# Sliding attention of a decoder layer: keys and values reversed by blocks, the sink as a 129th score, two output halves joined from PSUM

## The chip, the core and the metric

The kernel runs on one core of a Trainium2 chip. A core has five engines with a queue of instructions each: TensorE (PE, matrix products, with its weight loads listed as PEld), VectorE (DVE), ScalarE (ACT), GpSimd (POOL) and SyncE (SP), which here issues all DMA transfers. Each queue is worked off in order; an instruction whose data or buffer isn't ready holds those behind it. The metric is the time of one execution on the device, in microseconds.

## The reference, cut to what matters

One decoder layer, 1024 tokens, width 1024, everything in float32: a norm, input projections, two token mixers side by side (sliding attention and gated linear attention), gates, output projections, residual, norm. The change lies in the sliding attention, with 16 query heads of 64, 2 key heads, blocks of 128 queries and a window of 128:

```python
s = jnp.einsum('bnqhgd,bnkhd->bnhgqk', qb, keys).astype(jnp.float32) * (A_HEAD_DIM ** -0.5)
...
rel = qi + BLOCK - ki
band = (rel >= 0) & (rel < WINDOW)
valid = band[None] & ((blk > 0) | (ki >= BLOCK)[None])
s = jnp.where(valid[None, :, None, None], s, NEG_INF)
...
p = jax.nn.softmax(jnp.concatenate([s, sink], axis=-1), axis=-1)[..., :-1]
o = jnp.einsum('bnhgqk,bnkhd->bnqhgd', p.astype(v.dtype), vals)
```

`keys` holds 256 keys for a block of queries: those of the block before and its own. Of these, 128 are in the window of each query: for query q the own keys 0 to q, and q + 1 to 127 of the block before. Key 0 of the block before is in no query's window. The sink is one learned number per head that stands in the softmax's sum and has no value.

## The kernel before, in words

All products are float32 made of rounded parts: an operand x is h (x rounded) and l (the rest), and a product is h*h + h*l + l*h. The layer runs as one program: norm and transposes, projections that are parked in DRAM (in blocks of 512, on banks `sj`), then the sliding attention (the `with ExitStack() as c2` block, L564 to L734), then the gated linear attention, the output projections and the last norm. The order within each engine's queue is set when the program is built: a scheduler puts the instructions in an order by its own estimate of when each can start, so instructions of one unit of attention stand among projections and other units.

The attention works through 8 pairs of heads `i`. `prep` (L719) makes the next pair's queries and gates: weights come in by DMA, ACT rounds them to `wh` (L115), POOL subtracts to `wl` (L116), PE projects (`proj`, L132), POOL turns the queries (`rope`, L585 to L587), ACT and DVE split them into `qa`, `qb` (L639 to L642); `silu2` makes the gate `ag` (L293). `attend` (L645) then takes two halves `th` of 512 tokens, and in each two units `u` of two blocks `b`: 32 units in all. A unit is:

- PE: scores of two blocks for two heads into banks `sc` (three of them), 256 keys wide (L659). Queries carry h and l on the two halves of the partitions, keys are doubled.
- DVE: per block, a select that puts at each place after the query's the score of the block before (L665), in place in PSUM, and the maximum over the 128 places (L666).
- DVE: per block, nm = min(-max / 8, -sink) (L673) and nm + sink (L675), two columns each; ACT: the exponential of that (L676), and four exponentials of 128 scores with nm as bias, 1/8 as scale and a sum (L678).
- DVE: the sink's part is added to the sum (L680), and the reciprocal taken (L681). ACT scales two of the four score tiles (L685), DVE two (L687).
- PE: four transposes into the bank `pt` (one, L688). ACT rounds them to `ph` (L695), DVE subtracts to `pl` (L697), POOL masks both with the causal triangle to `ch` and `cl` (L696, L698).
- PE: the products with the values into `av` (two banks, L704). Values carry h on 64 output partitions and l on the other 64, so the result has two halves that must be added: ACT copies one (L707), DVE adds the other (L708), and DVE multiplies by 1/4 and the gate, one head at a time, into `oa` (L712), which goes to DRAM (L717).

With one key head for eight query heads, `kk[g]` holds the keys of head g, h and l, 1024 columns in the order of the tokens (L591 to L602). For the first block there is no block before, and the select takes -1e30.

Of the kernel before, what the change touches and what calls it, by code (L numbers as in the profile page):

```python
# [25 lines left out]
P = 128  # L26
# [31 lines left out]
def _turn_parts(k):  # L58
    """1/(2 pi) * 2**k modulo 1 as (multiple of 2**-12, rest)."""
    from fractions import Fraction  # L60

    pi = Fraction(314159265358979323846264338327950288419716939937510582097494459, 10**62)
    f = Fraction(2**k) / (2 * pi)
    f -= round(f)
    hi = Fraction(round(f * 4096), 4096)
    return float(hi), float(f - hi)
# [3 lines left out]
def layer_kernel(ctx: ExitStack, tc: tile.TileContext, consts, x, positions, norm_w, w_in, a_sinks,  # L70
# [56 lines left out]
    def half_product(p, w, m, start, stop):  # L127
        """p (+)= w^T m over 512 rows, both split."""
# [6 lines left out]
    def proj(w, m):  # L135
        """[128 columns of w, 512 tokens] of w^T m."""
# [20 lines left out]
    # hT[token half][row half]: (h, l)  # L157
# [109 lines left out]
    # the norm's weights, by head the same, with the factors of the queries and of the halves  # L267
# [19 lines left out]
    def silu2(pool, name, w, th, bufs=None):  # L287
        """2 silu of the projection's tile."""
# [65 lines left out]
    nsinks = const.tile([P, AH], F32, name="nsinks")  # L354
    nc.vector.tensor_scalar_mul(nsinks, sinks, -1.0)
# [5 lines left out]
    # the sums at the middle and end of the blocks  # L361
# [9 lines left out]
    # ---- pairs of column tiles over blocks of 512 x 512, seven half products instead of eight:  # L371
    # with W^T = [[a11, a12], [a21, a22]] by tile and row half, and the other operand in blocks bij,
    # s1 = a21 + a22, s2 = s1 - a11, s3 = a11 - a21, s4 = a12 - s2,
    # t1 = b12 - b11, t2 = b22 - t1, t3 = b22 - b12, t4 = b21 - t2,
    # u2 = a11 b11 + s2 t2, c11 = a11 b11 + a12 b21, c21 = u2 + s3 t3 + a22 t4,
    # c22 = u2 + s3 t3 + s1 t1, c12 = u2 + s1 t1 + s4 b22 ----
    slots = []

    def part(raw, n):
        """h and l of raw [P, 4, n]."""  # L380
# [12 lines left out]
    def token_product(p, w, m, t):  # L393
        """p = m^T w over 512 rows for token tile t of the half, both split."""
# [649 lines left out]
```

## Time and profile before

| | |
|---|---|
| time, median of 3 runs | 1153.88 us (1153.28 to 1154.51) |
| profiled execution, span (its own time isn't given apart) | 1153.5 us |
| busy in the span: PE, PEld, DVE, ACT, POOL | 1048.5, 885.6, 824.2, 535.7, 701.8 us |
| first select (L665) to the start of the last output product (L712) | 474.9 to 769.1 us |
| mean granted clock of PE | 0.969 |

The page of the profile gives busy times, 40 slices of the span, and groups of instructions as "line engine operation out<-in, shapes, count | busy us, mean ns | idle before, and who ended it". A view of one line adds "min/median/max" of the durations. A window's row gives the busy time of each engine in a stretch, with the number of instructions in brackets. In a timeline the columns are start, duration, engine, line. A wait's row names who waited for whom: total us, times, longest. A DVE instruction that stands blocked once it has started counts as busy all the while.

### The profile page before, as it was taken

The numbers are of one execution on the slowest core, as the hardware profiler recorded it, in microseconds if no ns is written. First come the engines' busy times: TensorE is split into PE (matmuls) and PEld (weight loads), VectorE is DVE, ScalarE is ACT, GpSimd is POOL, SyncE is SP. The second block draws the span as 40 slices with busy tenths as digits, with TensorE's granted clock in tenths as the row PEclk, the third lists the DMA queues.
The fourth block names the chain that finished last, engine by engine and source line by source line (L and its number), as shares of the span: only waits on it lengthen the run. The fifth ranks groups of instructions, "written<-read, shape, count | busy, mean of one in ns | idle before, by whom it ended". The sixth has DMA issues, their size and how long they took to land.

```text
span 1153.5 us, 16395 instructions
## 1 busy us (share of the span) xinstructions
PE 1048.5 (91%) x5544; PEld 885.6 (77%) x5544; DVE 824.2 (71%) x1386; ACT 535.7 (46%) x1248; POOL 701.8 (61%) x554
## 2 busy tenths in 40 slices
PE   5797999989999999988999899988999997994897
PEld 4575878878889997877777787767788885874896
DVE  6893688535564323699999899957866289899766
ACT  6236675333342214455555554636755143333444
POOL 4545455777996437657556675557845144679585
PEclk9998999999999999999999999998999998996998
DMA  6303443453334152221221213246764488641325
GB/s 223 92 32 114 143 146 128 146 181 103 111 116 123 63 151 61 64 65 37 83 83 46 56 56 108 85 137 195 246 190 136 137 269 244 181 137 55 104 62 182
DMA packets 126403, 141.07 MB, mean 122 GB/s; under 512 B 10352, under 2 KB 87024, under 8 KB 126320
## 3 DMA queue, kind: packets, MB, share of 16 engines
q1 hardware_dynamic: 126320, 140.03, 39.2%
q8 instruction: 44, 0.72, 0.3%
q14 instruction: 39, 0.32, 0.1%
HBM read 95.04 MB, written 40.24 MB: 117 GB/s over the span
## 4 chain that ended last, share of the span: by engine, by line
PE 39%; DVE 24%; issue 5%; POOL 5%; ACT 3%; DMA 3%; SPq 0%; POOLq 0%; DVEq 0%; ACTq 0%
PE pj L132 12%; PE sj L397 12%; PE sj L132 10%; DVE oa L712 3%; DVE nm L673 2%; DVE sm L687 2%; DVE mx L666 2%; DVE pl L697 2%; DVE sc L665 1%; POOL wl L116 1%; PE av L750 1%; DVE qa L641 1%; DVE qb L642 1%; DVE fo L708 1%; DVE den L680 1%
## 5 line engine op out<-in xcount | busy, mean ns | idle before, releaser
L132 PE MATMUL pj<-o,wh 128*128 128x512 f32 x1088 | 359.4, 405 | 9.3 <-DVE low L308 6.0
L132 PEld LDWEIGHTS pj<-o,wh 128*128 128x128 f32 x1088 | 205.1, 193 | 51.3 <-issue 6.4
L116 POOL TENSOR_TENSOR wl<-wr,wh 128x1024 fp32r<-128x1024 f32 (+1 forms) x76 | 164.7, 2177 | 113.1 <-ACT wh L115 106.7
L132 PE MATMUL pj<-o,wl 128*128 128x512 f32 x544 | 218.1, 401 | 0.0
L116 POOL TENSOR_TENSOR wl<-sraw,wh 128x512 fp32r<-128x512 f32 (+1 forms) x98 | 153.9, 1587 | 92.8 <-ACT wh L115 84.9
L132 PEld LDWEIGHTS pj<-o,wl 128*128 128x128 f32 x544 | 104.6, 192 | 21.4
L132 PE MATMUL sj<-o,wh 128*128 128x512 f32 x352 | 112.6, 401 | 5.0 <-ACT wh L115 4.8
L115 ACT CAST wh<-wr 128x1024 fp32r<-128x1024 f32 (+1 forms) x76 | 66.6, 889 | 93.0 <-PE pj L132 29.0
L428 DVE TENSOR_TENSOR u<-u,sj 128x512 f32<-128x512 f32 x72 | 49.1, 684 | 74.6 <-PE sj L132 37.0
L115 ACT CAST wh<-sraw 128x512 fp32r<-128x512 f32 (+1 forms) x98 | 63.2, 678 | 65.1 <-PE sj L397 29.9
L132 PEld LDWEIGHTS sj<-o,wh 128*128 128x128 f32 x352 | 67.2, 191 | 21.5 <-ACT wh L115 5.1
L678 ACT ACTIVATE sm<-sc,nm 128x128 f32<-128x128 f32 x128 | 46.1, 365 | 76.8 <-DVE nm L673 64.5
L397 PE MATMUL sj<-wh,b 128*128 128x256 f32 x320 | 63.8, 301 | 18.8 <-ACT b L881 9.2
L696 POOL TENSOR_TENSOR ch<-ph,cst 128x512 fp32r<-128x512 f32 x32 | 38.7, 1211 | 54.9 <-ACT ph L695 54.9
L132 PE MATMUL sj<-o,wl 128*128 128x512 f32 x176 | 70.4, 400 | 0.0
L397 PEld LDWEIGHTS sj<-wh,b 128*128 128x128 f32 x320 | 54.3, 208 | 20.2 <-ACT b L881 9.6
L132 PE MATMUL sj<-b,wh 128*128 128x512 f32 x160 | 50.7, 401 | 7.2 <-ACT wh L115 7.2
L397 PE MATMUL sj<-wh,o 128*128 128x256 f32 x320 | 57.3, 282 | 0.0
L698 POOL TENSOR_TENSOR cl<-pl,cst 128x512 fp32r<-128x512 f32 x32 | 38.5, 1202 | 18.1 <-DVE pl L697 9.8
L397 PEld LDWEIGHTS sj<-wh,o 128*128 128x128 f32 x320 | 49.3, 188 | 0.1
L397 PE MATMUL sj<-wl,b 128*128 128x256 f32 x160 | 46.5, 298 | 2.3 <-POOL wl L116 2.3
L585 POOL TENSOR_TENSOR qs<-qs,sin 128x512 f32<-128x512 f32 x18 | 24.2, 1343 | 35.5 <-DMA qs<-q 25.0
(313 smaller groups left out, 2823.5 us busy)
## 6 DMA issues: line engine op xcount, KB each, us to landing
sraw<-in_w_in_dram SPq DMA_DIRECT2D x32, 512.0 KB, 4.0
wr<-in_w_in_dram SPq DMA_DIRECT2D x26, 512.0 KB, 3.9
r<-sp_ob SPq DMA_DIRECT2D x28, 256.0 KB, 4.5
qs<-q SPq DMA_DIRECT2D x72, 64.0 KB, 2.0
xt<-in_x_dram SPq DMA_DIRECT2D x8, 512.0 KB, 8.2
sp_ma<-gt SPq DMA_DIRECT2D x16, 256.0 KB, 2.1
sp_mb<-c SPq DMA_DIRECT2D x16, 256.0 KB, 2.0
gt<-sp_cum SPq DMA_DIRECT2D x16, 256.0 KB, 3.6
```

The lines of the kernel that those rows point to most:

```text
L115: nc.scalar.copy(h, raw)
L116: nc.gpsimd.tensor_sub(l, raw, h.bitcast(F32))
L132: nc.tensor.matmul(p, a[:, k, :], b[:, k, :], start=start and k == 0 and y == 0, stop=stop and k == 3 and y == 2)
L397: nc.tensor.matmul(p, m[i][:, k, t * P : t * P + P], w[j][:, k, :], start=k == 0 and y == 0, stop=k == 3 and y == 2)
L428: nc.vector.tensor_add(o[b], like(u[b], o[b]), like(x[b], o[b]))
L585: nc.gpsimd.tensor_mul(qs, qs, sin[:, sl])
L666: nc.vector.reduce_max(mx[:, 2 * b : 2 * b + 2], own, axis=mybir.AxisListType.X)
L673: nc.vector.scalar_tensor_tensor(nm[:, 2 * b : 2 * b + 2], mx[:, 2 * b : 2 * b + 2], -0.125, nsinks[:, h0 : h0 + 2], ALU.mult, ALU.min)
L678: nc.scalar.activation(sm[:, j, :], sel[j // 2][:, j % 2, :], AF.Exp, bias=nm[:, j : j + 1], scale=0.125, accum_out=den[:, j : j + 1])
L696: nc.gpsimd.tensor_mul(ch, ph.bitcast(F32), leb)
L698: nc.gpsimd.tensor_mul(cl, pl.bitcast(F32), leb)
L712: nc.vector.scalar_tensor_tensor(oa[o : o + 64, u * 256 : u * 256 + 256].rearrange("p (b q) -> p b q", b=2), fv[:, :, h, :], 0.25, ag[o : ...
```

## The change

The program outside the attention is the same but for removed comments and a tile `nsinks` that is no longer made. In the attention:

- Keys are stored with 1/8 folded in, and last block first, with a ninth block of zeros behind (`kk` is 9 x 128 columns). The 256 columns that a unit reads are then the own block first and the block before behind it. The four zero blocks are cleared by POOL.
- The place of key 0 of the block before, column 128, which no query uses, takes the sink: ACT copies two numbers per partition into the score bank. Own block and sink are then 129 columns side by side.
- The select works on places 1 to 127 (place 0 is always the own key). One reduction takes minus the maximum over 129 columns, the exponential runs over 129 columns without a scale, and its sum holds the sink's part. The operations on two and four columns (L673, L675, L676, L680) are gone.
- The output: for each head ACT copies one half, times 1/4, from PSUM, and DVE multiplies the other half by 1/4 and adds, into a tile `fo` of 128 x 256; one product by the gate follows for both heads.

```diff
-        kk = [[(aps if g else ap0).tile([P, T], F32R, name=f"k{g}{x}") for x in "hl"] for g in range(AKV)]
+        kk = [[(aps if g else ap0).tile([P, NT + 1, P], F32R, name=f"k{g}{x}") for x in "hl"] for g in range(AKV)]
+        for g in range(AKV):
+            for y in range(2):
+                nc.gpsimd.memset(kk[g][y][:, NT, :].bitcast(F32), 0.0)
...
-            r = rope(w, th)
+            r = rope(w, th).rearrange("p (n t) -> p n t", n=4)[:, ::-1, :]
+            sl = slice(NT - 4 - th * 4, NT - th * 4)
...
-                    nc.scalar.copy(kk[g][0][o2 : o2 + 64, sl], r[o : o + 64, :])
+                    nc.scalar.activation(kk[g][0][o2 : o2 + 64, sl, :], r[o : o + 64], AF.Copy, scale=AD**-0.5)
...
-                    nc.vector.tensor_sub(kk[g][1][o2 : o2 + 64, sl], r[o : o + 64, :],
-                                         kk[g][0][o : o + 64, sl].bitcast(F32))
+                    nc.vector.scalar_tensor_tensor(kk[g][1][o2 : o2 + 64, sl, :], r[o : o + 64], AD**-0.5,
+                                                   kk[g][0][o : o + 64, sl, :].bitcast(F32), ALU.mult, ALU.subtract)
...
-                    k0 = max(n - 1, 0) * P
+                    k0 = NT - 1 - n
...
-                    sv = s.rearrange("p (h w j) -> p h w j", h=2, w=2)
-                    own = sv[:, :, min(n, 1), :]
-                    nc.vector.copy_predicated(own, up, sv[:, :, 0, :] if n else neg[:, :, None].to_broadcast([P, 2, P]))
-                    nc.vector.reduce_max(mx[:, 2 * b : 2 * b + 2], own, axis=mybir.AxisListType.X)
+                    sv = s.rearrange("p (h j) -> p h j", h=2)
+                    nc.scalar.copy(sv[:, :, P], sinks[:, h0 : h0 + 2])
+                    nc.vector.copy_predicated(sv[:, :, 1:P], up[:, :, 1:], sv[:, :, P + 1 :] if n else
+                                              neg[:, :, None].to_broadcast([P, 2, P - 1]))
+                    own = sv[:, :, : P + 1]
+                    nc.vector.tensor_reduce(nm[:, 2 * b : 2 * b + 2], own, axis=mybir.AxisListType.X,
+                                            op=ALU.max, negate=True)
...
-                for b in range(2):
-                    nc.vector.scalar_tensor_tensor(nm[:, 2 * b : 2 * b + 2], mx[:, 2 * b : 2 * b + 2], -0.125,
-                                                   nsinks[:, h0 : h0 + 2], ALU.mult, ALU.min)
-                    nc.vector.tensor_add(sk[:, 2 * b : 2 * b + 2], nm[:, 2 * b : 2 * b + 2], sinks[:, h0 : h0 + 2])
-                nc.scalar.activation(sk, sk, AF.Exp)
...
-                                         scale=0.125, accum_out=den[:, j : j + 1])
-                nc.vector.tensor_add(den, den, sk)
+                                         accum_out=den[:, j : j + 1])
...
-                fo = ap.tile([64, 512], F32, name="fo", bufs=2)
-                nc.scalar.copy(fo, av[64:128, :])
-                nc.vector.tensor_add(fo, av[0:64, :], fo)
-                fv = fo.rearrange("p (b h q) -> p b h q", b=2, h=2)
+                fo = ap.tile([P, 256], F32, name="fo", bufs=2)
+                avv = av.rearrange("p (b h q) -> p h b q", b=2, h=2)
+                fv = fo.rearrange("p (b q) -> p b q", b=2)
+                us = slice(u * 256, u * 256 + 256)
                 for h in range(2):
-                    o = h * 64
-                    nc.vector.scalar_tensor_tensor(
...
-                        ALU.mult, ALU.mult)
+                    o, o2 = slice(h * 64, h * 64 + 64), slice(64 - h * 64, P - h * 64)
+                    nc.scalar.activation(fv[o], avv[o2, h], AF.Copy, scale=0.25)
+                    nc.vector.scalar_tensor_tensor(fv[o], avv[o, h], 0.25, fv[o], ALU.mult, ALU.add)
+                nc.vector.tensor_mul(oa[:, us], fo, ag[:, us])
```

The scheduler makes a new order from this. On DVE, some way into the attention, a unit's work ran like this before (`sc` scores, `mx` maximum, `nm` minus the maximum, `sk` and `den` the sink's part and the sum, `sm` the probabilities, `pl` the rest of their rounding, `fo` and `oa` the output; lines as in the kernel before):

```order
L665 COPY_PREDICATED sc<-up,sc 128x2x128
L697 TENSOR_TENSOR pl<-pt,ph 128x512
L666 TENSOR_REDUCE mx<-sc 128x2
L673 SCALAR_TENSOR_TENSOR nm<-mx,nsinks 128x2
L675 TENSOR_TENSOR sk<-nm,sinks 128x2
L708 TENSOR_TENSOR fo<-av,fo 64x512
L712 SCALAR_TENSOR_TENSOR oa<-fo,ag 64x256 x2
L680 TENSOR_TENSOR den<-den,sk 128x4
L293 SCALAR_TENSOR_TENSOR ag<-gt,pj 128x512
L681 RECIPROCAL den<-den 128x4
L687 TENSOR_SCALAR sm<-sm,den 128x128 x2
L697 TENSOR_TENSOR pl<-pt,ph 128x512
```

And now, about as far along in DVE's queue of the changed kernel (L671 select, L674 maximum, L713 multiply-add of the halves, L714 product by the gate, L680 reciprocal, L686 scaling, L696 subtraction for `pl`):

```order
L671 COPY_PREDICATED sc<-up,sc 128x2x127
L713 SCALAR_TENSOR_TENSOR fo<-av,fo 64x256
L674 TENSOR_REDUCE nm<-sc 128x2
L713 SCALAR_TENSOR_TENSOR fo<-av,fo 64x256
L714 TENSOR_TENSOR oa<-fo,ag 128x256
L680 RECIPROCAL den<-den 128x4
L686 TENSOR_SCALAR sm<-sm,den 128x128 x2
L293 SCALAR_TENSOR_TENSOR ag<-gt,pj 128x512
L696 TENSOR_TENSOR pl<-pt,ph 128x512
```

The maximum itself is what ACT waits for now; nothing stands between it and the exponential, nor between sum and reciprocal. The output's two multiply-adds stand apart, with a maximum between them.

On ACT, for a unit inside the attention, with what each waits for in brackets (an engine's or a DMA queue's semaphore), before (`ph` the rounded probabilities, L707 the copy of the output half, L291 the gate):

```order
L707 COPY fo<-av 64x512 [waits PE_49]
L695 CAST ph<-pt 128x512 [waits PE_49]
L678 ACTIVATE sm,den<-sc,nm 128x128 [waits DVE_49,Activation_49]
L678 ACTIVATE sm,den<-sc,nm 128x128
L678 ACTIVATE sm,den<-sc,nm 128x128 [waits DVE_49]
L678 ACTIVATE sm,den<-sc,nm 128x128
L291 ACTIVATE gt<-pj 128x512 [waits PE_49]
L676 ACTIVATE sk<-sk 128x4 [waits DVE_49]
L685 ACTIVATE sm<-sm,den 128x128 [waits DVE_49,Activation_49]
L685 ACTIVATE sm<-sm,den 128x128 [waits Activation_49]
```

And now (L670 the sink's copy into the score bank, L712 the copy of an output half, L684 the scaling, L694 the rounding):

```order
L670 COPY sc<-sinks 128x2 [waits PE_49]
L712 ACTIVATE fo<-av 64x256 [waits PE_49]
L678 ACTIVATE sm,den<-sc,nm 128x129 [waits DVE_49,Activation_49]
L678 ACTIVATE sm,den<-sc,nm 128x129
L291 ACTIVATE gt<-pj 128x512 [waits PE_49]
L712 ACTIVATE fo<-av 64x256 [waits DVE_49]
L678 ACTIVATE sm,den<-sc,nm 128x129 [waits DVE_49,Activation_49]
L678 ACTIVATE sm,den<-sc,nm 128x129
L684 ACTIVATE sm<-sm,den 128x128 [waits DVE_49]
L684 ACTIVATE sm<-sm,den 128x128 [waits Activation_49]
L694 CAST ph<-pt 128x512 [waits PE_49]
```

The sink's copy waits for PE's scores and stands ahead of what follows in the queue, and the second half's copy waits for DVE, whose multiply-add of the first half is to be done with the bank.

More of the change, by code (lines that the diff above doesn't have):

```diff
@@ L352, in layer_kernel @@
             nc.sync.dma_start(sp_rope[i, :, g * 256 : g * 256 + 256], trig[i][g * 32 : g * 32 + 32, :])
-    nsinks = const.tile([P, AH], F32, name="nsinks")
-    nc.vector.tensor_scalar_mul(nsinks, sinks, -1.0)
     caus = const.tile([P, P], I32, name="caus")
@@ L588, in rope @@
             return q
-        kk = [[(aps if g else ap0).tile([P, T], F32R, name=f"k{g}{x}") for x in "hl"] for g in range(AKV)]
+        kk = [[(aps if g else ap0).tile([P, NT + 1, P], F32R, name=f"k{g}{x}") for x in "hl"] for g in range(AKV)]
+        for g in range(AKV):
+            for y in range(2):
+                nc.gpsimd.memset(kk[g][y][:, NT, :].bitcast(F32), 0.0)
         w = wtile(w_in, O_AK)
         for th in range(TH):
-            sl = slice(th * 512, th * 512 + 512)
-            r = rope(w, th)
+            r = rope(w, th).rearrange("p (n t) -> p n t", n=4)[:, ::-1, :]
+            sl = slice(NT - 4 - th * 4, NT - th * 4)
             for g in range(AKV):
@@ L649, in attend @@
             for u in range(2):
-                mx = ap.tile([P, 4], F32, name="mx")
+                nm = ap.tile([P, 4], F32, name="nm")
+                den = ap.tile([P, 4], F32, name="den")
+                sm = ap.tile([P, 4, P + 1], F32, name="sm", bufs=2)
                 sel = []
@@ L658, in attend @@
                         for x in range(2):
-                            nc.tensor.matmul(s[:, h * 256 : h * 256 + 256], lq, kk[kv][x][:, k0 : k0 + 256],
+                            nc.tensor.matmul(s[:, h * 256 : h * 256 + 256], lq,
+                                             kk[kv][x][:, k0 : k0 + 2, :].rearrange("p n t -> p (n t)"),
                                              start=x == 0, stop=x == 1)
-                    sv = s.rearrange("p (h w j) -> p h w j", h=2, w=2)
-                    own = sv[:, :, min(n, 1), :]
@@ L665, in attend @@
-                    nc.vector.copy_predicated(own, up, sv[:, :, 0, :] if n else neg[:, :, None].to_broadcast([P, 2, P]))
-                    nc.vector.reduce_max(mx[:, 2 * b : 2 * b + 2], own, axis=mybir.AxisListType.X)
-                    sel.append(own)
-                nm = ap.tile([P, 4], F32, name="nm")
-                sk = ap.tile([P, 4], F32, name="sk")
-                den = ap.tile([P, 4], F32, name="den")
-                sm = ap.tile([P, 4, P], F32, name="sm", bufs=2)
-                for b in range(2):
-                    nc.vector.scalar_tensor_tensor(nm[:, 2 * b : 2 * b + 2], mx[:, 2 * b : 2 * b + 2], -0.125,
-                                                   nsinks[:, h0 : h0 + 2], ALU.mult, ALU.min)
-                    nc.vector.tensor_add(sk[:, 2 * b : 2 * b + 2], nm[:, 2 * b : 2 * b + 2], sinks[:, h0 : h0 + 2])
@@ L684, in attend @@
                     if j < 2:
-                        nc.scalar.activation(sm[:, j, :], sm[:, j, :], AF.Copy, scale=den[:, j : j + 1])
+                        nc.scalar.activation(sm[:, j, :P], sm[:, j, :P], AF.Copy, scale=den[:, j : j + 1])
                     else:
-                        nc.vector.tensor_scalar_mul(sm[:, j, :], sm[:, j, :], den[:, j : j + 1])
-                    nc.tensor.transpose(pt[:, j * P : j * P + P], sm[:, j, :], ident)
+                        nc.vector.tensor_scalar_mul(sm[:, j, :P], sm[:, j, :P], den[:, j : j + 1])
+                    nc.tensor.transpose(pt[:, j * P : j * P + P], sm[:, j, :P], ident)
                 parts = [ap.tile([P, 4, P], F32R, name=nm_, bufs=2) for nm_ in ("ph", "pl", "ch", "cl")]
```

3 lines of the change are left out of this document (removed).

## The prediction

> **What bounds the kernel now.** I read the page's 40 slices first, then the stage in which the changed lines run (476 to 770 us) beside two stretches in which PE is full, then the groups of DVE in that stage, single lines, and two places in the timeline.
>
> ```profile
> PE   5797999989999999988999899988999997994897
> DVE  6893688535564323699999899957866289899766
> core 0: us, PE busy (x) PEld busy (x) DVE busy (x) ACT busy (x) POOL busy (x), PEclk, DMA share, GB/s
> 280.00:320.00 40.00, 40.00 (x176) 32.73 (x175) 22.74 (x31) 15.57 (x29) 33.83 (x23) 1.00 0.35 114
> 360.00:400.00 40.00, 40.00 (x338) 40.00 (x337) 14.36 (x18) 9.60 (x11) 17.62 (x8) 1.00 0.33 104
> 476.00:770.00 294.00, 267.54 (x1396) 220.38 (x1395) 265.04 (x561) 160.53 (x496) 176.65 (x130) 0.99 0.24 71
> ```
>
> A slice is 28.8 us; from the 18th slice to the 26th DVE stands at 8 or 9 tenths. The stage has 294 us; DVE is busy in 265.0 of them (90%), PE in 267.5 (91%), so the page alone does not say which of the two sets the time. Two more views do: the chain that ended last, asked for this stage alone, and the waits.
>
> ```profile
> by line: DVE oa L712 12.6%; DVE nm L673 7.9%; DVE sm L687 7.8%; PE pj L132 7.2%; DVE mx L666 6.4%; DVE pl L697 6.2%; issue 6.0%; DVE sc L665 5.8%; DVE qa L641 5.0%; DVE qb L642 4.9%; DVE fo L708 4.7%; DVE den L680 4.6%; DVE sk L675 4.5%; DV
> ACT sm L678 <- DVE nm L673: 64.5, 32, 4.9
> ACT sm L685 <- DVE den L681: 25.3, 16, 3.3
> PE av L704 <- ACT ph L695: 9.9, 8, 3.0
> PE pt L688 <- DVE pl L697: 6.3, 7, 2.3
> ```
>
> Eleven of the thirteen entries that can be read in the chain are DVE's, PE's projections have 7.2%, and the longest wait (64.5 us, 32 times) is ACT waiting for a maximum that DVE makes. DVE sets this stage.
>
> How much room PE has is a matter of how it is read. In a full stretch 176 matmuls 512 columns wide take 40.00 us, 0.227 us each, and 338 that are 256 wide 0.118 us each. Four transposes follow each other like this:
>
> ```profile
> 571.11 0.60 PE L688 MATMUL pt<-cst,sm 128*128 128x128 f32 x4
> 571.46 0.48 PE L132 MATMUL pj<-o,wh 128*128 128x512 f32 x1
> L132 PE MATMUL pj<-o,wh 128*128 128x512 f32 x522 | 171.5, 401 | 0.1
> L132 PE MATMUL pj<-o,wl 128*128 128x512 f32 x262 | 104.5, 399 | 0.0
> L688 PE MATMUL pt<-cst,sm 128*128 128x128 f32 x128 | 24.5, 287 | 10.7 <-DVE pl L697 6.3 <-DVE sm L687 3.2 <-ACT sm L685 0.9
> ```
>
> The next matmul starts 0.35 us after the first of the four: 0.088 us each. The stage's 1396 PE instructions are 784 wide ones (522 + 262), 128 transposes and 484 others, all 256 wide: 784 x 0.227 + 484 x 0.118 + 128 x 0.088 = 178.2 + 57.3 + 11.2 = 246.7 us. So PE needs 247 of the 294 us, and 47 us is the most that the stage can give.
>
> Weighed against a page: the busy column leaves PE only 26.5 us of room (294 - 267.5), the starts leave 47, because a matmul's bar is longer than the distance to the next. The Trainium skill (Perfetto Trace Analysis, Identifying the Most-Contended Engine) calls matmul busy time no good measure and takes the share of weight loads instead; these are busy 220.4 of 294 us here (75%) and 32.7 to 40.0 of 40 where PE is full, so the trace sides with it. By the busy column the forecast below would be 26.5 - 20.6 = 6 us of gain and 1148 us.
>
> **What DVE's time consists of.** Its groups in the stage that the change touches, then their spread (min/median/max, ns):
>
> ```profile
> L712 DVE SCALAR_TENSOR_TENSOR oa<-fo,ag 64x256 f32<-64x256 f32 x64 | 41.4, 647 | 0.7
> L687 DVE TENSOR_SCALAR sm<-sm,den 128x128 f32<-128x128 f32 x64 | 32.4, 547 | 0.8
> L673 DVE SCALAR_TENSOR_TENSOR nm<-mx,nsinks 128x2 f32<-128x2 f32 x64 | 27.1, 427 | 0.8
> L675 DVE TENSOR_TENSOR sk<-nm,sinks 128x2 f32<-128x2 f32 x64 | 24.6, 390 | 0.5
> L708 DVE TENSOR_TENSOR fo<-av,fo 64x512 f32<-64x512 f32 x32 | 21.6, 675 | 7.9 <-ACT fo L707 7.7
> L680 DVE TENSOR_TENSOR den<-den,sk 128x4 f32<-128x4 f32 x32 | 15.3, 478 | 5.7 <-ACT sk L676 5.1
> L641 DVE TENSOR_TENSOR qa<-q,qa 64x512 fp32r<-64x512 f32 x14 | 14.7, 1049 | 2.6 <-ACT qa L639 2.2
> L673 DVE SCALAR_TENSOR_TENSOR nm<-mx,nsinks x64: 124/160/2284, 477.4 to 751.7; 128x2 f32<-128x2 f32 x64
> L675 DVE TENSOR_TENSOR sk<-nm,sinks x64: 137/160/2366, 477.9 to 753.7; 128x2 f32<-128x2 f32 x64
> L680 DVE TENSOR_TENSOR den<-den,sk x32: 145/164/2369, 479.6 to 754.8; 128x4 f32<-128x4 f32 x32
> L687 DVE TENSOR_SCALAR sm<-sm,den x64: 270/286/2431, 480.1 to 756.6; 128x128 f32<-128x128 f32 x64
> L712 DVE SCALAR_TENSOR_TENSOR oa<-fo,ag x64: 402/422/1789, 499.2 to 769.1; 64x256 f32<-64x256 f32 x64
> L708 DVE TENSOR_TENSOR fo<-av,fo x32: 652/674/683, 498.0 to 767.9; 64x512 f32<-64x512 f32 x32
> 564.51 2.41 POOL L116 TENSOR_TENSOR wl<-wr,wh 128x1024 fp32r<-128x1024 f32 x1 [1.41 <-ACT wh L115]
> 564.57 2.37 DVE L675 TENSOR_TENSOR sk<-nm,sinks 128x2 f32<-128x2 f32 x1
> ```
>
> The maximum over two columns takes 0.16 us as a rule and up to 2.28. The last two rows show why: an addition of two columns stands for 2.37 us while POOL runs a 2.41 us subtraction, and ends with it. The operations with this spread read SBUF alone; the one that reads PSUM (L708) has none (652 to 683 ns).
>
> **The change part by part.** *Gone:* the 160 small operations, 27.1 + 24.6 + 15.3 = 67.0 us of DVE, of which 41.4 are waits for POOL (mean less median, times the count: 16.9 + 14.4 + 10.1). They stood in the chain between maximum and exponential and between sum and reciprocal.
>
> *The output.* The addition of halves (21.6) and the two products (41.4) go, 63.0 us. In their place come 64 multiply-adds of 64x256 that read PSUM and one SBUF tile, and 32 products of 128x256 from SBUF. The first I take at L712's median, 0.422 us (same shape, no waits, as L708 has none): 27.0 us; the dear end is L708's 0.675 for twice the columns: 43.2. The second I take at L712's mean, 0.647, waits and all, since it too reads two SBUF tiles: 20.7; ends 0.422 (13.5) and L641's mean 1.049 (33.6).
>
> The select has two forms in the trace:
>
> ```profile
> L665 DVE COPY_PREDICATED sc<-up,sc x56: 410/420/430, 476.1 to 743.9; 128x256 f32<-128x256 int32 x56
> L665 DVE COPY_PREDICATED_SCALAR sc<-up,neg x8: 471/484/489, 474.9 to 725.2; 128x256 f32 x8
> ```
>
> *Select and maximum over 254 and 129 columns instead of 256 and 128*, from an odd column of PSUM: taken as 0, since no row has such a start. The ends come from these two forms: 64 x (0.484 - 0.420) = 4 us either way.
>
> DVE's sum: 265.0 - 67.0 - 63.0 + 27.0 + 20.7 = 182.7 us. That is well under PE's 246.7, so DVE stops being the bound and PE is late next.
>
> *ACT.* The exponential of the sinks goes, the copy of halves is cut in two, and 64 copies of two columns into the score bank come.
>
> ```profile
> L676 ACT ACTIVATE sk<-sk 128x4 f32<-128x4 f32 x32 | 6.6, 205 | 10.2 <-DVE sk L675 10.1
> L707 ACT COPY fo<-av 64x512 f32<-64x512 f32 x32 | 18.7, 584 | 7.8 <-PE av L704 7.1
> ```
>
> A sink copy I take at L676's 0.205 us (nearest in size; the dear end is L707's 0.584): 13.1 us. A half of the output at 256 columns lies between the two rows, 0.39 us: 25.1. ACT goes from 160.5 to 160.5 - 6.6 - 18.7 + 13.1 + 25.1 = 173.4 us, two thirds of the new stage. The copies are also a new wait: ACT stands until PE has made the scores, with exponentials, casts and weight roundings queued behind it, and DVE's select now waits for ACT.
>
> *Keys.* The factor 1/8 rides on a copy and a subtraction that were there. Four clears of 128 columns come into POOL's queue between the first two weight subtractions of the attention:
>
> ```profile
> L753 POOL MEMSET att<- x4: 204/204/206, 741.9 to 742.3; 128x128 f32 x4
> 419.25 2.38 POOL L116 TENSOR_TENSOR wl<-wr,wh 128x1024 fp32r<-128x1024 f32 x1 [3.09 <-ACT wh L115]
> ```
>
> A clear of that shape takes 0.204 us, and ahead of the second subtraction POOL idles 3.09 us, which covers four (0.8 us, the price without the cover). If they had to wait for their place in SBUF, the subtraction behind them would be late by that wait less 3.09 us.
>
> *What stays on PE's path.* DVE's scalings ahead of the transposes (L687) keep their waits for POOL, 32.4 - 64 x 0.286 = 14.1 us, and PE, which works in order, waits with it. Half of the sink copies' 13.1 us I put on the path too, the other half beside projections: 6.5. So the stage becomes 246.7 + 20.6 = 267.3 us and the gain is 294 - 267.3 = 26.7 us. PE's work elsewhere, the loads and the later stages stay as they are and move up by that. Span 1153.5, median of the three runs 1153.88: the profiled execution is a typical one, and 1153.9 - 26.7 = 1127.2, said as 1127.
>
> **The rivals.**
>
> *The waits for POOL stay (20%).* POOL's work is unchanged, so the 41.4 us may only move to the next operation that reads SBUF; with both dear ends DVE has 265.0 - 130.0 + 43.2 + 33.6 + 41.4 = 253.2 us, and at its present 90% density the stage is 281 us: gain 13, 1141 us, up to 1150 with some of the new waits. For it: POOL is busy 176.7 of 294. Against: 160 of the operations that could wait are gone, and the new ones mostly read PSUM.
>
> *ACT and DVE hand each other every bank in turn (9%), slower.* Before, a score bank went PE, DVE, ACT; now PE, ACT, DVE, ACT. And the output bank goes ACT, DVE, ACT, DVE: the second half's copy waits in ACT's queue for DVE's first multiply-add. The Trainium skill (PSUM — Partial Sum Buffer, PSUM bank collisions raise a hardware error) states that two engines must not even read one bank's quadrant at once, which is why that chain can't be loosened; no run here shows a collision. That makes 64 + 32 = 96 new waits in ACT's queue. At the 2.0 us that a wait for the maximum takes now (64.5 / 32) they are worth 193 us on 173.4; it decides from (294 - 173.4) / 96 = 1.26 us each, and at 1.5 the stage has 173.4 + 144 = 317 us: 1177. Against: those 2.0 us come from a DVE that is never free, and it would be.
>
> *PE was the bound all along (5%), no change, 1154.* For it: 91% busy, and 9.9 us of PE's waits end with a cast by ACT. Against: the chain, and PE's starts.
>
> **How the numbers follow.** My forecast (66%) is 1127, with its own range from 1110 (PE within 3 us of its floor, as between 280 and 320) to 1137 (the remainder of 20.6 half as large again, 31 us). With the first rival the range reaches 1150; what lies outside is the slower case, no change and a little at each end. A measurement of this kernel tells about 0.2% (2.3 us) from no change. Faster: 66 + 20 = 86%; the same 5%; slower 9%.
>
> **What would show it.** DVE's busy time in the stage at 170 to 205 us; the two columns' groups gone; multiply-adds of the output with a spread like L708's; scalings still spread to 2 us; PE's busy column above 95% and the distance between first select and last output product near 267 us. Wrong: DVE still above 230 us (waits moved), or ACT idle ahead of the sink copies or the second half's copy above 100 us in total (hand-over), or PE idle as much as now with DVE half free.

## The result and the profile after

| | before | after |
|---|---|---|
| time, median (lowest to highest, runs) | 1153.58 us (1150.82 to 1154.51, 4) | 1123.83 us (1122.53 to 1126.03, 4) |
| ratio, 95% interval | | 0.9732 [0.9711, 0.9753] |
| profiled span | 1153.5 us | 1120.8 us |
| first select to the start of the last output product | 474.9 to 769.1: 294.2 us | 474.9 to 737.7: 262.8 us |

The changed kernel is faster by 29.8 us. The stage is shorter by 31.4 us and starts when it did, so the gain is made in the stage. (Of what the title names, the keys alone are reversed; the values keep their order.) The slices of PE and DVE in the changed kernel (28.0 us each), and its row for the stage:

```profile
PE   4797999989999999999999999988999998994896
DVE  6894687554565422378888888748765199899766
```

```profile
474.90:737.70 262.80, 259.01 (x1408) 219.14 (x1407) 212.01 (x400) 166.40 (x557) 177.32 (x130) 1.00 0.27 80
```

From the 18th slice to the 26th PE now stands at 9 throughout and DVE at 7 or 8. PE is busy in 259.0 of 262.8 us (98.6%, before 91%), DVE in 212.0 (81%, before 90%). The chain that ended last in the stage has changed its owner, and the longest waits have shrunk:

```profile
by line: PE pj L132 34.2%; PE av L703 6.4%; PE sc L663 5.9%; issue 5.2%; ACT sm L678 3.7%; DVE qa L643 3.3%; DVE sc L671 2.8%; PE pt L687 2.8%; DVE qb L644 2.8%; DVE nm L674 2.3%; DMA qs<-q 2.3%; DVE fo L713 2.2%; DVE sm L686 2.1%; DVE oa L
```

```profile
ACT sm L678 <- DVE nm L674: 35.6, 25, 7.4
ACT fo L712 <- DVE fo L713: 21.9, 17, 3.8
DVE fo L713 <- ACT fo L712: 20.0, 22, 4.8
ACT sm L684 <- DVE den L680: 8.0, 12, 2.1
DVE sc L671 <- ACT sc L670: 4.1, 4, 2.1
PE av L703 <- ACT ph L694: 1.6, 3, 1.0
PE pt L687 <- DVE pl L696: 1.1, 1, 1.1
PE pt L687 <- DVE sm L686: 0.4, 1, 0.4
```

PE's projections, 7.2% of the chain before, are 34.2% of it. ACT waits 35.6 us for a maximum instead of 64.5, and 8.0 for a reciprocal instead of 25.3. The last three rows are what PE itself waits for; with 0.7 us for a gate's operation on ACT they come to 3.8 us in all. The groups of DVE that matter, and the spread of single lines (min/median/max in ns):

```profile
L686 DVE TENSOR_SCALAR sm<-sm,den 128x128 f32<-128x128 f32 x64 | 36.0, 604 | 0.8
L713 DVE SCALAR_TENSOR_TENSOR fo<-av,fo 64x256 f32<-64x256 f32 x64 | 26.8, 419 | 21.0 <-ACT fo L712 20.0
L714 DVE TENSOR_TENSOR oa<-fo,ag 128x256 f32<-128x256 f32 x32 | 22.2, 694 | 0.8
L644 DVE TENSOR_TENSOR qb<-q,qb 64x512 fp32r<-64x512 f32 x14 | 21.0, 1503 | 0.4
L643 DVE TENSOR_TENSOR qa<-q,qa 64x512 fp32r<-64x512 f32 x14 | 20.5, 1468 | 7.0 <-ACT qa L641 6.7
```

```profile
L713 DVE SCALAR_TENSOR_TENSOR fo<-av,fo x64: 402/422/429, 495.1 to 737.3; 64x256 f32<-64x256 f32 x64
L714 DVE TENSOR_TENSOR oa<-fo,ag x32: 393/426/1508, 497.0 to 737.7; 128x256 f32<-128x256 f32 x32
L686 DVE TENSOR_SCALAR sm<-sm,den x64: 274/289/1334, 478.2 to 725.3; 128x128 f32<-128x128 f32 x64
L671 DVE COPY_PREDICATED sc<-up,sc x56: 405/418/428, 475.3 to 718.1; 128x254 f32<-128x254 int32 x56
L670 ACT COPY sc<-sinks x64: 149/163/193, 472.6 to 714.2; 128x2 f32<-128x2 f32 x64
L712 ACT ACTIVATE fo<-av x64: 375/378/383, 491.9 to 736.9; 64x256 f32<-64x256 f32 x64
L593 POOL MEMSET k0h<- x1: 204/204/204, 417.5 to 417.5; 128x128 f32 x1
L593 POOL MEMSET k1l<- x1: 206/206/206, 418.0 to 418.0; 128x128 f32 x1
```

The multiply-add from PSUM (L713) has no spread at all. The operations that take all their tensors from SBUF still have one, and the splitting of the queries (L643, L644) has grown from a mean of 1.05 us to 1.47 and 1.50. There the waits for POOL come up again: 26 of the 32 splits take more than 0.8 us, and each of these ends 0.54 to 0.55 us after the end of an operation of POOL.

### The profile page after: what moved, and what is told of

Read it like the earlier page. It is cut to its first block, busy times and chain, and to the rows that moved or that the text cites. A ratio compares the mean times of both kernels' runs of the same rounds, so it can differ in the third digit from the quotient of the medians.

```text
span 1120.8 us, 16315 instructions
## 1 busy us (share of the span) xinstructions
PE 1035.0 (92%) x5544; PEld 877.8 (78%) x5544; DVE 765.8 (68%) x1225; ACT 542.4 (48%) x1312; POOL 705.5 (63%) x558
## 4 chain that ended last, share of the span: by engine, by line
PE 57%; DVE 14%; POOL 10%; issue 6%; DMA 5%; ACT 5%; SPq 2%; POOLq 0%; DVEq 0%; ACTq 0%
PE sj L132 21%; PE pj L132 15%; PE sj L395 11%; POOL wl L116 3%; POOL b L880 2%; PE av L748 2%; PE av L703 1%; PE sc L663 1%; DMA r<-sp_ob 1%; POOL o L880 1%; DVE qa L643 1%; ACT sm L678 1%; POOL q L585 1%; DMA oraw<-sp_oa 1%; PE sc L748 1%
## 5 line engine op out<-in xcount | busy, mean ns | idle before, releaser
L395 PE MATMUL sj<-wh,b 128*128 128x256 f32 x320 | 62.5, 297 | 21.4 <-ACT b L879 14.4
L395 PEld LDWEIGHTS sj<-wh,b 128*128 128x128 f32 x320 | 53.0, 204 | 22.8 <-ACT b L879 14.8
L678 ACT ACTIVATE sm<-sc,nm 128x129 f32<-128x129 f32 x128 | 45.8, 368 | 36.7 <-DVE nm L674 35.6
L395 PE MATMUL sj<-wl,o 128*128 128x256 f32 x160 | 44.2, 277 | 0.0
```

Of the source, the lines that this page charges most:

```text
L395: nc.tensor.matmul(p, m[i][:, k, t * P : t * P + P], w[j][:, k, :], start=k == 0 and y == 0, stop=k == 3 and y == 2)
L678: nc.scalar.activation(sm[:, j, :], sel[j // 2][:, j % 2, :], AF.Exp, bias=nm[:, j : j + 1], accum_out=den[:, j : j + 1])
```

## The experiments

**The theories.** The prediction's theory (A): DVE's time, waits for POOL counted in, sets the stage until PE's floor is reached. Against it stand these. The place matters (B): what costs is a wait, or a link, in the chain from scores to exponentials, however busy DVE is. The hand-over of banks between ACT and DVE costs. PE set the time all along. The last runs call A's and B's cores theory 1 (waits) and theory 2 (each operation, each link).

For each run the stage is taken from its own first select to its own last output product. PE's floor is worked out as in the prediction from that stage's matmuls (512 wide at 0.227 us, 256 wide at 0.118, 128 wide at 0.088; 8 or 16 that are 64 wide stand in four of the stages and are put in at 0.06, an estimate), and "lost" is the stage less the floor. The 0.227 us prove a little low for this stage, by some 5 us in the sum, in every row alike. Some expectations count the stage from the select's other form, which starts 0.4 to 1.2 us later. Ratios are to the kernel before, run on the same chip beside it.

| kernel | median us | ratio [95%] | stage | PE floor | PE lost | DVE busy |
|---|---|---|---|---|---|---|
| before | 1153.58 | 1 | 294.2 | 246.6 | 47.6 | 265.7 |
| changed | 1123.83 | 0.9732 [0.9711, 0.9753] | 262.8 | 249.1 | 13.7 | 212.0 |
| sink part alone | 1133.82 | 0.9817 [0.9792, 0.9841] | 273.5 | 249.3 | 24.2 | 228.1 |
| output part alone | 1146.04 | 0.9942 [0.9912, 0.9972] | 285.3 | 250.0 | 35.3 | 252.0 |
| before, pointer scalars | 1150.64 | 0.9971 [0.9953, 0.9989] | 287.8 | 253.6 | 34.2 | 269.3 |
| before + 4th pass | 1162.91 | 1.0074 [1.0059, 1.0090] | 302.4 | 279.6 | 22.8 | 266.4 |
| changed + 4th pass | 1143.35 | 0.9907 [0.9891, 0.9924] | 284.8 | 275.2 | 9.6 | 198.9 |
| sink copy on DVE | 1125.47 | 0.9728 [0.9690, 0.9766] | 262.7 | 248.8 | 13.9 | 223.5 |
| two-input pairs beside | 1135.43 | 0.9844 [0.9824, 0.9865] | 275.1 | 249.3 | 25.8 | 234.9 |
| one-input beside | 1123.07 | 0.9733 [0.9707, 0.9758] | 261.8 | 249.1 | 12.7 | 206.7 |
| one-input in the stage | 1113.91 | 0.9655 [0.9634, 0.9675] | 256.7 | 246.6 | 10.1 | 219.1 |
| two-input in the chain | 1164.67 | 1.0088 [1.0062, 1.0114] | 306.9 | 250.8 | 56.1 | 246.7 |
| one-input in the chain | 1132.16 | 0.9814 [0.9789, 0.9839] | 275.0 | 250.8 | 24.2 | 226.0 |
| all scalings on ACT | 1121.94 | 0.9721 [0.9699, 0.9744] | 263.1 | 252.2 | 10.9 | 175.9 |

One thing limits all comparisons. The scheduler sets the order anew for every program, so an edit also moves instructions that it doesn't touch. How much that may be worth shows below, where a kernel with more work is 10 us faster.

### Each part alone

The sink part alone is the changed kernel with the output of before (ACT copies one half, DVE adds, two products); the output part alone is the kernel before with the joined output.

```diff
-                    nc.scalar.activation(fv[o], avv[o2, h], AF.Copy, scale=0.25)
-                    nc.vector.scalar_tensor_tensor(fv[o], avv[o, h], 0.25, fv[o], ALU.mult, ALU.add)
-                nc.vector.tensor_mul(oa[:, us], fo, ag[:, us])
+                nc.scalar.copy(fo, av[64:128, :])
+                nc.vector.tensor_add(fo, av[0:64, :], fo)
...
```

> The changed kernel with the output of before (one copy by ACT, one addition, two products by the gate). Theory A (DVE's time set the stage, PE sets it now): DVE gets back 63.0 us of groups for 49.0, its groups in the stage go from 223 to about 237 of 263 us, so it is near the bound again: 5 to 12 us slower than the changed kernel, 1129 to 1136. Theory B (the links taken out between maximum and exponential, and between sum and reciprocal, made the gain, not DVE's time): the chain is as short as in the changed kernel, 1123 to 1126. Theory C (the joined output made half of the gain or more): 1139 or more.

> The kernel before with the joined output alone. Theory A: DVE's groups lose 14 of 288 us, the stage about 10 to 15: 1139 to 1145. Theory B: no link between maximum and exponential is gone, so no change, 1152 to 1155. Theory C: half of the gain or more, 1139 or less. If the exchange of the output bank between ACT and DVE costs something where DVE is full: 1156 or more.

The sink part takes 20.7 us off (1154.48 to 1133.82, medians of runs on one chip), inside A's range. The output part takes 8.4 off, 3 to 10 by its interval; 1146.04 is 1 us above A's range and clear of B's. In the stage the steps add up in either order: 294.2 to 273.5 to 262.8 (20.7 and 10.7), or 294.2 to 285.3 to 262.8 (8.9 and 22.5). So the sink part is about two thirds of the gain. The output part's 8.9 and 10.7 us are no more than a new order of the instructions may be worth (see below); that they agree in two different orders speaks for them. The group of output products with the sink part alone:

```profile
L712 DVE SCALAR_TENSOR_TENSOR oa<-fo,ag 64x256 f32<-64x256 f32 x63 | 55.6, 882 | 0.8
```

Its mean is 0.882 us, before 0.647, while the shape is the same. Over the undisturbed 0.422 that is 64 x 0.460 = 29.4 us of waits in place of 14.4: 15 us of waits more, against the 41.4 that went with the small operations. With the output joined, 32 products are left, and the waits in them are 32 x (0.694 - 0.426) = 8.6 us.

### The small operations of before without their waits

In the kernel before, nm and its sum with the sink are computed in one-column pieces, 256 operations that read one SBUF tensor and a scalar per partition, in place of 128.

```diff
-                for b in range(2):
-                    nc.vector.scalar_tensor_tensor(nm...
+                for j in range(4):
+                    c, hj = slice(j, j + 1), h0 + j % 2
+                    nc.vector.tensor_scalar(nm[:, c], mx[:, c], -0.125, nsinks[:, hj : hj + 1], ALU.mult, ALU.min)
+                    nc.vector.tensor_scalar(sk[:, c], nm[:, c], sinks[:, hj : hj + 1], None, ALU.add)
```

> The kernel before, where each of the two-column operations on maximum and sink (one input from SBUF beside another) is made as two operations on one column with the sink as a scalar per partition: 256 operations in place of 128, same chain, two links longer. If the price of these operations was their wait for POOL, and such an operation has no such wait: 256 x 0.14 = 36 us in place of 51.7, stage 10 to 15 us shorter, 1138 to 1145. If the price was their number or the length of the chain (theory B): 1158 to 1170. If operations with one input wait for POOL as the scalings do (0.25 us each on top): 1180 or more.

```profile
L674 DVE TENSOR_SCALAR nm<-mx,nsinks x128: 193/204/217, 478.9 to 746.5; 128x1 f32<-128x1 f32 x128
L675 DVE TENSOR_SCALAR sk<-nm,sinks x128: 176/204/216, 479.7 to 748.2; 128x1 f32<-128x1 f32 x128
```

The waits are gone from both lines (longest 217 ns, before 2366), but 256 x 0.204 = 52.2 us stand where 27.1 + 24.6 = 51.7 stood, so DVE is as busy as before. PE loses 13 us less in the stage; the time falls by 3.8 us only, and 1150.64 lies between the ranges, 6 us above the one for waits. The stage holds 25 more wide matmuls (5.7 us) in this order, so it is shorter by 6.4 us only, and it starts 1.5 us later. The run shows that the form of the operation decides about the wait. It also shows that a kernel without these waits gains little while DVE's busy time stays (269.3 of 287.8 us).

### Was PE the bound?

A fourth pass (l x l) in the gates' projections adds 128 matmuls 512 wide, 29.1 us of PE, to each kernel.

```diff
-                for y, (a, b) in enumerate(((w[0], m[0]), (w[0], m[1]), (w[1], m[0]))):
+                passes = [(w[0], m[0]), (w[0], m[1]), (w[1], m[0])] + [(w[1], m[1])] * more
+                for y, (a, b) in enumerate(passes):
...
-        p = proj(w, hT[th])
+        p = proj(w, hT[th], True)
```

> The kernel before with a fourth pass (l*l) in the 16 gate projections of the attention: 128 matmuls of 512 columns more on PE, 128 x 0.227 = 29.1 us, of which an eighth lies ahead of the stage; DVE, ACT and POOL have nothing more to do. Theory A: PE needs 247 + 25 = 272 of 294 us, so most of it goes into its idle time: 1156 to 1165. If PE was the bound all along: 1180 to 1184.

> The changed kernel with the same fourth pass. Theory A: PE sets the stage now, so nearly all of 29.1 us shows: 1148 to 1154. If DVE, POOL or the chain still set it: 1124 to 1138.

```profile
472.90:775.30 302.40, 292.31 (x1547) 245.42 (x1546) 266.42 (x561) 160.89 (x498) 176.83 (x131) 1.00 0.24 70
```

```profile
475.50:760.30 284.80, 283.97 (x1523) 240.95 (x1522) 198.85 (x402) 168.18 (x557) 178.29 (x131) 1.00 0.25 73
```

In the kernel before (first row) the floor of the stage rises by 33.0 us and the stage by 8.2; the time rises by 8.2. In the changed kernel (second row) the floor rises by 26.1, the stage by 22.0 and the time by 19.5, with PE busy 283.97 of 284.80 us. (The rest of the pass lies outside the stage.) The first run came as theory A said. The second is 5 us below A's range and 5 above the other: 4.1 of the 26.1 us went into gaps that PE still had. Before, PE had room for three quarters of the extra work, so it was not the bound; after, little room is left. That settles the rival by which PE set the time all along.

### Does the hand-over of banks cost?

The sink copy goes from ACT to DVE, so that a score bank passes from PE to DVE as before, and 64 waits of ACT go.

```diff
-                    nc.scalar.copy(sv[:, :, P], sinks[:, h0 : h0 + 2])
+                    nc.vector.tensor_copy(sv[:, :, P], sinks[:, h0 : h0 + 2])
```

> The changed kernel with the sink's copy into the score bank on DVE instead of ACT: no hand-over from ACT ahead of the select. Theory A: DVE gets 64 x 0.1 to 0.16 us more and loses 4.1 us of waits, with time to spare: 1121 to 1127, no difference beyond 3 us. If the hand-over costs time that shows: 1119 or less. If DVE is still near its limit: 1128 or more.

```profile
L670 DVE COPY sc<-sinks x64: 140/153/165, 475.8 to 716.1; 128x2 f32<-128x2 f32 x64
```

The ratio is 0.9728 [0.9690, 0.9766] against 0.9732 [0.9711, 0.9753]: no difference, with PE losing 13.9 us against 13.7. So the sink copies' hand-over costs nothing that can be measured, within some 4 us by the interval. It also shows 11.5 us more of DVE that don't lengthen the stage, since DVE is no longer the bound. The output bank's hand-over was not taken out by itself; the output part alone, with all of it, is faster.

### Number or waits?

Three kernels add operations into tiles that nobody reads. The first adds two-input additions behind each maximum and each set of exponentials, the second reciprocals at the same places.

```diff
+                    nc.vector.tensor_add(d1[:, 2 * b : 2 * b + 2], sinks[:, h0 : h0 + 2], sinks[:, h0 : h0 + 2])
+                    nc.vector.tensor_add(d2[:, 2 * b : 2 * b + 2], nm[:, 2 * b : 2 * b + 2], sinks[:, h0 : h0 + 2])
...
+                nc.vector.tensor_add(d3, den, d2)
```

> The changed kernel with as many small DVE operations as were taken out (64 + 64 on two columns, 32 on four, two SBUF inputs each), written to tiles that nobody reads: beside the chain. Theory A: DVE's groups go from 223 to 270 to 290 of 263 us, it is the bound again: 1139 to 1149. Theory B (the chain's links): nothing waits for them, 1123 to 1127.

> The same 160 operations beside the chain with one SBUF input each (reciprocals, 0.17 us, which have no wait for POOL in the trace of before). Theory A: DVE's groups go up by 27 us at most to 250 of 263: 1125 to 1133, and clearly faster than with two inputs. If the number of instructions and not the waits for POOL was the price: as slow as with two inputs.

The pairs cost 11.6 us, between the ranges of A and B; the reciprocals cost none, 2 us below A's range. The two look like a clean pair, and are not. In the trace of the second, the reciprocals of the sinks don't lie in the stage:

```profile
L677 DVE RECIPROCAL d<-sinks x64: 142/144/158, 423.3 to 431.1; 128x2 f32<-128x2 f32 x64
L678 DVE RECIPROCAL d<-sinks x64: 141/144/151, 423.4 to 431.2; 128x2 f32<-128x2 f32 x64
```

They read nothing that is made late, so the scheduler put all 128 at 423 to 431 us, ahead of the stage; of the pairs' 160 it put 64 there. In the stage stood 96 pairs against 32 reciprocals. A third kernel keeps 96 one-input operations in the stage, by having them read the maxima:

```diff
+                    nc.vector.reciprocal(d2[:, 2 * b : 2 * b + 2], nm[:, 2 * b : 2 * b + 2])
...
+                nc.vector.reciprocal(d3, den)
```

> The changed kernel with 96 added operations of DVE that read one SBUF tile and stay in the stage: a reciprocal of two columns of the negated maximum behind each maximum (64) and one of the four sums behind each set of exponentials (32), into tiles that nobody reads. It is the counterpart of the 96 two-input additions that lay in the stage in the earlier run with pairs beside the chain (stage 274.7 us, 11.9 more than the changed kernel). At 0.145 and 0.177 us they are 15.0 us of DVE. Theory 1 (waits for POOL cost, the number of operations doesn't): stage 262 to 266 us, time 1122 to 1127 us. Theory 2 (each small operation costs whatever it reads): stage 271 to 277 us, time 1132 to 1138 us.

The 64 pairs that read the maxima, then the 64 reciprocals that do:

```profile
L678 DVE TENSOR_TENSOR d<-nm,sinks x64: 139/160/1247, 477.9 to 736.3; 128x2 f32<-128x2 f32 x64
```

```profile
L677 DVE RECIPROCAL d<-nm x64: 128/158/167, 475.2 to 716.7; 128x2 f32<-128x2 f32 x64
```

With the same number at nearly the same undisturbed length, PE loses 25.8 us beside the pairs and 10.1 beside the reciprocals. But the reciprocals' kernel is 10 us faster than the changed kernel itself, below both theories' ranges, and useless work is an unlikely cause of that. What else differs is the order: with the two traces laid side by side, 1578 of the 5544 matmuls have one of another shape or tile in their place. So the order may be worth some 10 us here. Of the 10.5 us that the span (1110.3 us) is shorter, 6.1 lie in the stage, where PE loses 3.6 us less and 11 wide matmuls fewer stand, 1.7 ahead of it and 2.7 behind. That the order is the cause is inferred; a kernel with the same order and without the reciprocals was not run, and with all scalings on ACT (below) 1413 matmuls stand elsewhere and the time is the same. The pairs' 12 us are hardly more than these 10, and don't decide.

### The place in the chain

The same kinds of operation now stand in the chain and leave the values as they are: two behind each maximum, ahead of the exponentials, and one ahead of each reciprocal, 160 in all. In the first kernel they add zeros from a tile (two SBUF inputs), in the second they take the maximum over an axis of one element (one input).

```diff
+                    nc.vector.tensor_tensor(d1[:, 2 * b : 2 * b + 2], nx[:, 2 * b : 2 * b + 2], zero2, ALU.add)
+                    nc.vector.tensor_tensor(nm[:, 2 * b : 2 * b + 2], d1[:, 2 * b : 2 * b + 2], zero2, ALU.add)
...
+                nc.vector.tensor_tensor(den, den, zero4, ALU.add)
```

```diff
+                    nc.vector.tensor_reduce(d1[:, 2 * b : 2 * b + 2], nx[:, 2 * b : 2 * b + 2, None],
+                                            axis=mybir.AxisListType.X, op=ALU.max)
...
```

> The changed kernel with 160 small operations of two SBUF inputs put back into the chain: minus the maximum takes two additions of zero before the exponential may use it, the sum one before the reciprocal. Theory A: as with the operations beside the chain, 1139 to 1150. Theory B: the whole gain is gone but for the output's part, 1148 or more, and far slower than beside the chain.

> The changed kernel with 160 added operations of DVE in the chain, at the places of the earlier run with two-input additions in the chain (stage 306.5 us, 1164.7 us), but each reads one SBUF tile: a maximum over an axis of one element, so the values stay. Two more links of about 0.15 us between maximum and exponentials, for each bank, and one between sums and reciprocal, 25 us of DVE in all. Theory 1 (what costs in the chain are the waits for POOL): the stage is 8 to 20 us over the changed kernel's 262.8, so 271 to 283 us, time 1132 to 1144 us. Theory 2 (what costs is a longer chain, since each link passes through a queue in order): stage 295 to 310 us, time 1153 to 1168 us.

In these two programs every instruction of every engine stands at the same place (the first only clears one more tile at the start), so the order is no part of their difference. The two-input links, their scalings and the wait behind them, then the same of the one-input kernel:

```profile
L680 DVE TENSOR_TENSOR d<-d,zero x64: 144/161/1261, 479.2 to 766.5; 128x2 f32<-128x2 f32 x64
L681 DVE TENSOR_TENSOR nm<-d,zero x64: 141/157/2346, 479.4 to 766.7; 128x2 f32<-128x2 f32 x64
L686 DVE TENSOR_TENSOR den<-den,zero x32: 149/164/2364, 481.2 to 768.4; 128x4 f32<-128x4 f32 x32
```

```profile
L681 DVE TENSOR_TENSOR nm<-d,zero 128x2 f32<-128x2 f32 x64 | 28.8, 467 | 0.3
L680 DVE TENSOR_TENSOR d<-d,zero 128x2 f32<-128x2 f32 x64 | 26.8, 436 | 0.6
L693 DVE TENSOR_SCALAR sm<-sm,den 128x128 f32<-128x128 f32 x64 | 24.0, 418 | 1.1
L686 DVE TENSOR_TENSOR den<-den,zero 128x4 f32<-128x4 f32 x32 | 11.2, 350 | 19.8 <-ACT sm L684 19.8
```

```profile
ACT sm L684 <- DVE nm L681: 70.0, 21, 8.0
```

```profile
L677 DVE TENSOR_REDUCE d<-d x64: 135/148/156, 477.9 to 735.0; 128x2 f32<-128x2 f32 x64
L679 DVE TENSOR_REDUCE nm<-d x64: 133/145/157, 478.1 to 735.2; 128x2 f32<-128x2 f32 x64
L685 DVE TENSOR_REDUCE den<-den x32: 143/157/159, 479.9 to 736.9; 128x4 f32<-128x4 f32 x32
```

```profile
L692 DVE TENSOR_SCALAR sm<-sm,den 128x128 f32<-128x128 f32 x64 | 42.6, 708 | 1.1
```

```profile
ACT sm L683 <- DVE nm L679: 49.8, 22, 7.3
```

Undisturbed, a link takes 0.145 to 0.164 us in both. The two-input links wait 64 x (0.436 - 0.161) + 64 x (0.467 - 0.157) + 32 x (0.350 - 0.164) = 43.4 us in all, the one-input links not at all. The difference is 31.9 us of the stage and 32.5 us of the time: with waits the kernel is slower than before, without them it keeps most of the gain and lies at the lower end of theory 1's range. The two-input kernel is 15 us above A's range and in B's.

Of the waits themselves a part only moves: with one-input links the scalings wait 64 x (0.708 - 0.290) = 26.8 us, with two-input links 64 x (0.418 - 0.287) = 8.4. So DVE's busy time differs by 20.7 us, the stage by 31.9, and DVE is busy in no more than 80% and 82% of the two stages. A wait costs more in these links than in the scalings: ACT stands 70.0 us for the maxima instead of 49.8, with the exponentials and all that is queued behind them, and PE loses 56.1 us instead of 24.2. Here A alone falls short and B's core is shown, for waits. As to length by itself, 160 links without waits cost 8.3 us against the changed kernel, which is within what the order can make, so that stays open.

### All scalings on ACT

```diff
-                    if j < 2:
-                        nc.scalar.activation(sm[:, j, :P], sm[:, j, :P], AF.Copy, scale=den[:, j : j + 1])
-                    else:
-                        nc.vector.tensor_scalar_mul(sm[:, j, :P], sm[:, j, :P], den[:, j : j + 1])
+                    nc.scalar.activation(sm[:, j, :P], sm[:, j, :P], AF.Copy, scale=den[:, j : j + 1])
```

> The changed kernel with all four scalings of a set on ACT (two were on DVE, 36.0 us with 17 us of waits for POOL). ACT takes 64 more of 0.406 us, 26 us: busy 166.4 becomes 192 of some 260 us. The floor of PE's starts is 249.7 us of the stage's 262.8. If what PE still loses (13 us) goes back to DVE's waits ahead of the transposes: stage 254 to 259 us, time 1115 to 1120 us. If ACT's queue takes their place (it stands between scores, exponentials, casts and copies): stage 263 to 272 us, time 1124 to 1133 us.

```profile
473.60:736.70 263.10, 262.77 (x1436) 223.28 (x1435) 175.92 (x344) 186.35 (x628) 178.97 (x131) 1.00 0.28 80
```

DVE is free of 36 us and ACT has 20 more, and the time is that of the changed kernel (the intervals overlap nearly whole), between the two expectations. PE loses 10.9 us instead of 13.7, and 8 more wide matmuls lie in the stage. So the scalings' waits for POOL on DVE cost no more than the 20 us of work that took their place on ACT; that they were hidden fits PE's 0.4 us of waits for them, but the run alone doesn't show it.

The fastest kernel that was run is the one with reciprocals in the stage, 1113.91 us. Its extra operations are useless, so it points to the order as the next thing to try, rather than to itself.

## Why the prediction was right

**PE next: right. DVE as the bound: right, but not by its sum alone.** With DVE relieved the chain went to PE, PE's busy share to 98.6%, and the fourth pass shows both halves, room before and little after. That DVE's busy time counts is borne out by the pointer scalars, which take waits away and leave that time and nearly all of the kernel's as they were. But the two-input links in the chain make a kernel slower than before with DVE busy in 80% of its stage (before 90%), so where DVE's waits stand counted as well. The 1127 forecast stands 3 us from the measured 1123.8, and the stage at 262.8 us against 267.3.

**The floor: right in its count, some 5 us low in its price (see the next point).** 246.7 us was foreseen, 249.1 came, as 11 more wide matmuls lie in the shorter stage.

**What stays on PE's path: wrong in its parts, near in size by luck.** 20.6 us were put there and 13.7 came. The 14.1 us were to be the scalings' waits for POOL, and PE's matmuls wait 0.4 us for a scaling in all; with the scalings on ACT the time is the same. The 6.5 us were half of the sink copies, and with these on DVE PE loses as much. A part of the 13.7 us isn't loss at all. The 0.227 us of a wide matmul came from earlier projections, on banks `sj`. These three pieces of the changed kernel's chain hold nothing but projections of the stage, on banks `pj`:

```profile
673.05 4.66 PE pj L132 x20
704.64 4.89 PE pj L132 x21
728.50 5.61 PE pj L132 x24
```

That is 0.233 to 0.234 us each, at the same granted clock of 1.00 as between 280 and 320 us, so the 796 wide matmuls take some 5 us more than the floor says; why, no run shows. PE's waits in the profile come to 3.8 us, and to 0.2 us with the scalings on ACT, where 10.9 count as lost. So the waits that were to stay on PE's path hardly came about, a floor that was too low stood in for a part of them, and that the stage came out only 4.5 us shorter than said (6.9 less lost, 2.4 more floor) is partly luck.

**DVE's sum: mis-sized.** 182.7 us were worked out and 212.0 came, outside the 170 to 205 that was to show the step right, though under the 230 that would have shown it wrong. There are two reasons. First, the durations of a stage's groups were subtracted from its busy time, but bars of neighbours overlap: before, all of DVE's groups in the stage add up to 288.3 us where 265.0 are busy. Second, waits moved. By groups, 288.3 - 67.0 - 63.0 + 27.0 + 20.7 = 206.0 was to be expected, and the groups after add up to 223.3. Of the 17.3 us more, the splits (L643, L644) carry 5.8 and 5.4, the scalings 3.6 and the products 1.5. So the first rival was right on the mechanism: most of these 17 us are waits that came up elsewhere, against the 41.4 that went. It decided nothing, since the sum stayed below PE's floor.

**The terms of the output: right.** 27.0 us for the multiply-adds (26.8), 20.7 for the products (22.2), 25.1 for ACT's halves (24.2). The select's new form cost nothing (0.418 us against 0.420). A sink copy took 0.163 us, not 0.205; ACT's total came to 166.4 instead of 173.4. The four clears took 0.205 each, ahead of a subtraction that had room.

**The hand-over: right to leave it at a small chance.** It was to decide from 1.26 us for each of 96 waits. In the output bank ACT waited for DVE 17 times, 21.9 us, 1.29 each, but 17 are not 96; the sink copies waited for the scores 5 times, 2.2 us, and DVE's select for a sink copy 4 times, 4.1 us. The price came about and the number didn't.

**What the prediction left out.** It gave all of DVE's microseconds the same worth. The pair in the chain shows that they are not: the small operations between maximum and exponential were a worse place for waits than the scalings. This bears on the sink part, two thirds of the gain. The order, which may be worth some 10 us, was not in the range's reasons either; how much of the 29.8 us it made, no run shows.

## What to carry over

In this kernel, where DVE and POOL work side by side, a tiny operation was dear if it took two tensors from SBUF and stood between two engines: fold such a one into the reduction or the activation next to it, or give it a form that reads one. Don't add up waits without asking who stands behind them: 43 us of waits cost 32 us between maximum, exponential and reciprocal, while PE stood 0.4 us for the 20 us in the scalings. And where a scheduler sets the order, an experiment needs a partner with the same order; a pair of programs that differ in one operation's form gave the one clean answer here.

## What the runs showed of the hardware

Which operations of DVE waited while POOL worked, by the spread of their durations (min/median/max in ns). With a spread up to 2.4 us: additions with two tensors from SBUF (137/160/2366 in the kernel before, L675), and the scaling of 128 columns by a number per partition (277/290/2437 with one-input links in the chain, L692). Without: reciprocals (128/158/167 with one-input operations in the stage) and reductions (133/145/157 in the chain) of a few columns from SBUF, the form with pointer scalars on one column (193/204/217), and the multiply-add with one tensor from PSUM (402/422/429 in the changed kernel). The Trainium skill (SBUF — State Buffer, Who interferes with whom) says that DVE and GpSimd share a pair of ports held by one at a time, that an operation with two SBUF inputs needs it against a GpSimd operation that reads SBUF, and one with a single input outside the two-port modes doesn't. The durations above agree with the rule for one and for two inputs. The page counts the scaling among the forms that can enter such a mode; here that form waited at 128 columns and not at one.

That 160 one-input operations in the chain cost 8.3 us where 160 two-input operations cost 40.8, and that 96 useless reciprocals stood in the fastest kernel, had not been expected: the number of instructions on DVE, at 0.15 us each, counted for little against their form and place.
